# Larger units and larger DMA descriptors in a streaming log-sum-exp scan

## The chip, the cores and the metric

The kernel runs on one core of a Trainium2 chip. The metric is the device time of one execution in microseconds (us); the six runs of the kernel before lie within 0.14% of one another (1250.54 to 1252.28). A profile of one execution is read beside the times.

## The reference

```python
# x: (8, 4096, 2048) float32
out[:, 0, :] = x[:, 0, :]
for t in range(1, 4096):
    mx = np.maximum(out[:, t-1, :], x[:, t, :])
    out[:, t, :] = mx + np.log(np.exp(out[:, t-1, :] - mx) + np.exp(x[:, t, :] - mx))
```

It is a running log-sum-exp along the second axis: 268 MB are read and 268 MB are written. The kernel computes exp, a prefix sum, and log.

## The kernel before: the parts that matter

A tile is 512 rows: 128 partitions, each with R = 4 consecutive rows of 2048 floats, so one partition's share is 32 KiB, contiguous in HBM. The profile shows one DMA packet for each such share (65 loads of 128 data packets and 16 small ones, under 512 B, are the 9360 of queue q1; the small ones come at the end of a transfer and are called its completion packets below); the text below calls its size the descriptor size. There are NI = 6 buffers.

```python
R = 4;  NI = 6
ti = [pool.tile([P, R, D], f32, name=f"ti{i}", tag=f"ti{i}") for i in range(NI)]
...
# SyncE: a buffer is loaded again when its store has landed
take(sp, stored[n], 16)
load(x_v[bass.ds(j * NI + n, 1)][0], n)
...
# ScalarE, tile by tile: exp of tile n, then log of tile n-1, then its store
exp(n, 0);  exp(n, 1)                    # two halves of the columns
ln(n - 1, 0, ...);  ln(n - 1, 1, ...)
store(n - 1, ...)
...
# VectorE: adds row r-1 to row r inside each partition (3 adds a half);
# PE: sums over partitions and the carry from the tile before, into PSUM;
# VectorE: adds that PSUM row to all four rows
```

Loads are issued by SyncE on one DMA queue (q1 in the profile), stores by ScalarE on another (q10). The logarithm of tile n-1, and with it the store, comes after the exponential of tile n, and so after the landing of the load of tile n.

The softmax here doesn't subtract the row's maximum and nothing guards it: scores larger than these inputs give would overflow.

## Time and profile before

| | before |
|---|---|
| median of 6 runs | 1250.79 us |
| share of DMA queues q1 + q10 | 49.9% + 49.9% |
| VectorE / ScalarE / PE busy | 82% / 73% / 52% |
| one tile in the steady state | 19.40 us |
| load / store, issue to landing | 38.4 / 44.0 us |

The lines themselves stand in the prediction. In a group line, the two numbers after the first bar are the total busy time in us and the mean of one instruction in ns; after the second bar come the engine's idle time before them and what ended it. A queue's share is the time that its packets took, as a share of 16 engines over the span.

### The profile page before, as it was taken

The page shows a single profiled execution, that of the slowest core. Times are in us where ns is not written, and L with a number is a line of the kernel's source. Part 1 is how long each engine was busy: PE and PEld are TensorE (multiplying, and loading weights), DVE is VectorE, ACT ScalarE, POOL GpSimd, SP SyncE. Part 2 cuts the span into 40 slices and gives each one's busy share as a digit, 9 for nine tenths or more (in the row PEclk, how much of TensorE's full clock was granted, in tenths as well). Part 3 has the DMA queues.
Part 4 walks back from the last instruction along what each step waited for, and adds up shares of the span by engine and source line. Part 5 has one row for each costly group of instructions (what it writes and reads, how often), then busy time and mean ns, then how long its engine had stood idle before and what let it go on. Part 6 is the DMA issues. An engine that isn't in the chain of part 4 may idle for free. (4 is left out here: it accounts for less than half of the span.)

```text
span 1249.0 us, 3456 instructions
## 1 busy us (share of the span) xinstructions
PE 650.8 (52%) x960; PEld 215.3 (17%) x960; DVE 1023.0 (82%) x512; ACT 907.2 (73%) x258; POOL 1.1 (0%) x8
## 2 busy tenths in 40 slices
PE   3556455554566545655455544565545564465541
PEld 1112111111112111211111111121111121111110
DVE  4999978778787787887878878778787787877873
ACT  5897866867768677686776866867768677686774
POOL 0000000000000000000000000000000000000000
PEclk9897778786887868778778786777878878678785
DMA  9999999999999999999999999999999999999998
GB/s 403 420 436 430 433 430 437 433 431 434 430 436 434 431 433 430 437 434 430 434 430 436 436 430 434 430 436 437 428 434 431 436 436 429 434 430 436 436 430 354
DMA packets 20409, 537.01 MB, mean 430 GB/s; under 512 B 2096, under 2 KB 2096, under 8 KB 4144
## 3 DMA queue, kind: packets, MB, share of 16 engines
q1 hardware_dynamic: 9360, 268.44, 49.9%
q10 hardware_dynamic: 11040, 268.44, 49.9%
q8 instruction: 7, 0.11, 0.0%
q14 instruction: 2, 0.02, 0.0%
HBM read 268.44 MB, written 268.44 MB: 430 GB/s over the span
## 5 line engine op out<-in xcount | busy, mean ns | idle before, releaser
L136 ACT ACTIVATE ti<-ti 128x4096 f32<-128x4096 f32 (+1 forms) x128 | 452.6, 3582 | 310.2 <-ACTq L59 304.2
L232 DVE TENSOR_TENSOR ti<-ti 128x1024 f32<-128x1024 f32 x384 | 464.7, 1224 | 200.0 <-ACT ti L136 191.3
L241 DVE TENSOR_TENSOR ti<-ti,ps 128x4096 f32<-128x4096 f32 x128 | 560.0, 4416 | 9.4 <-PE ps L208 9.0
L208 PE MATMUL ps<-ti,before 128*128 128x512 f32 x512 | 380.4, 895 | 342.6 <-DVE ti L232 342.1
L142 ACT ACTIVATE ti<-ti 128x4096 f32<-128x4096 f32 x128 | 455.4, 3602 | 11.5 <-PE ps L197 6.0
L197 PE MATMUL ps<-ti,last 128*128 128x512 f32 x448 | 270.6, 735 | 234.2 <-DVE ti L241 234.2
L208 PEld LDWEIGHTS ps<-ti,before 128*128 128x128 f32 x512 | 128.7, 279 | 609.0 <-DVE ti L232 500.9
L197 PEld LDWEIGHTS ps<-ti,last 128*128 128x128 f32 x448 | 86.6, 214 | 401.8 <-DVE ti L241 334.7
L159 ACT ACTIVATE ti<-ti 128x4096 f32<-128x4096 f32 x1 | 3.6, 3616 | 6.5 <-ACTq L59 6.5
L32 ACT ACT_TABLE_LOAD x1 | 1.3, 1283 | 0.8 <-PEq L274 0.8
L103 POOL TENSOR_SCALAR_AFFINE_SELECT last<-last 128x128 f32<-128x128 f32 x1 | 0.3, 296 | 0.0
L98 POOL TENSOR_SCALAR_AFFINE_SELECT before<-before 128x128 f32<-128x128 f32 x1 | 0.3, 295 | 0.1
L95 POOL MEMSET last<- 128x128 f32 x1 | 0.2, 206 | 0.0
L94 POOL MEMSET before<- 128x128 f32 x1 | 0.2, 205 | 0.5 <-SPq L77 0.5
L274 POOL MEMSET const-bfloat16-1.0<- 128x1 bf16 x1 | 0.1, 103 | 0.0
L274 POOL MEMSET const-uint8-127<- 128x1 uint8 x1 | 0.1, 103 | 0.0
L274 POOL MEMSET const-float32-0.0<- 128x1 f32 x1 | 0.1, 99 | 0.3 <-issue 0.3
L274 POOL MEMSET const-float32-1.0<- 128x1 f32 x1 | 0.1, 99 | 0.0
## 6 DMA issues: line engine op xcount, KB each, us to landing
ti<-in_x_dram SPq DMA_DIRECT2D x63, 4096.0 KB, 38.4
out_dram<-ti ACTq DMA_DIRECT2D x62, 4096.0 KB, 44.0
out_dram<-ti ACTq DMA_DIRECT2D x4, 2048.0 KB, 12.9
ti<-in_x_dram SPq DMA_DIRECT2D x2, 2048.0 KB, 9.7
```

Of the source, the lines that this page charges most:

```text
L32: nc.scalar.preload_act_table_set("natural_log_exp_and_others")
L94: g.memset(before[:], 1.0).then_inc(ones, 1)
L98: g.affine_select(out=before[:], in_=before[:], compare_op=mybir.AluOpType.is_ge, fill=0.0, base=-1, pattern=[[1, P]], channel_multiplier= ...
L103: g.affine_select(out=last[:], in_=last[:], compare_op=mybir.AluOpType.is_ge, fill=0.0, base=-(P - 1), pattern=[[0, P]], channel_multiplier=1,
L136: act.activation(t[:, rows, half(h)], t[:, rows, half(h)], ACT.Exp).then_inc(exps[h], 1)
L142: act.activation(t[:, :, half(h)], t[:, :, half(h)], ACT.Ln)._wait_ge(carried[h], turn + 1).then_inc(logs, 1)
L159: act.activation(ti[0][:, 0:2, :], ti[0][:, 0:2, :], ACT.Exp)
L197: m = pe.matmul(ps[(n + 1) % 2][:, sl], last[:], ti[n % NI][:, R - 1, sl], start=True, stop=False, skip_group_check=True,)
L208: m = pe.matmul(ps[n % 2][:, sl], before[:], ti[n % NI][:, R - 1, sl], start=n % NBLK == 0, stop=True, skip_group_check=True,)
L232: a = dve.tensor_add(t[:, r, half(h)], t[:, r - 1, half(h)], t[:, r, half(h)])
L241: dve.tensor_add(t[:, :, half(h)], t[:, :, half(h)], ps[n % 2][:, half(h)].unsqueeze(1).to_broadcast([P, R, HALF]),)._wait_ge(ahead[h], n ...
L274: nc = _bacc.Bacc("TRN2", target_bir_lowering=False, num_devices=1)
```

## The change

The intent: units of 1024 rows (eight to a partition) make one partition's share 64 KiB, so that loads and stores need half as many descriptors and semaphore waits. The six buffers become three of twice the size. Only the first four and the last four units have 512 rows. Loops are unrolled on every engine. The first two large units store in two pieces, to free their halves earlier. The core of the diff:

```diff
-    R = 4
-    NI = 6
+    SLOTS, R = 6, 4
+    HEAD, SPLIT, TAIL = 4, 2, 4
+    while row < B * S:
+        r = R if len(units) < HEAD or row >= B * S - TAIL * R * P else 2 * R
+        units.append((row // S, row % S, r, slot))
...
-    ti = [pool.tile([P, R, D], f32, name=f"ti{i}", tag=f"ti{i}") for i in range(NI)]
+    big = [pool.tile([P, 2 * R, D], f32, name=f"big{i}", tag=f"big{i}") for i in range(SLOTS // 2)]
...
+                for u in range(N):
+                    first, _, free = fills[u]
+                    for k, n in free:
+                        sp.wait_ge(stored[k], n)
+                    r = units[u][2]
...
+                        sp.dma_start(
+                            out=sbuf(u, slice(0, r), full), in_=dram(x, u)
+                        ).then_inc(loaded[first], 16)
...
+                for u in range(N):
+                    if u < N - 1:
+                        for h in range(2):
+                            exp(u + 1, h)
+                    ln(u, 0, slice(0, units[u][2]))
+                    own = slots(u)
+                    for i, rows in enumerate(parts(u)):
+                        ln(u, 1, rows)
+                        store(u, rows, stored[own[i % len(own)]])
```

There are 36 units: 4 small, 28 large, 4 small. ScalarE's order is unchanged.

More of the change, by code (lines that the diff above doesn't have):

```diff
@@ L35 @@
     P = 128
-    R = 4
-    NBLK = S // (P * R)
-    NT = B * NBLK
+    SLOTS, R = 6, 4
     FD = 512
-    NI = 6
     HALF = D // 2
-    assert NI % 2 == 0 and NBLK % 2 == 0 and D == 4 * FD
+    HEAD, SPLIT, TAIL = 4, 2, 4
+    assert D == 4 * FD and HEAD % 2 == 0 and TAIL % 2 == 0
+    units = []
+    row = slot = 0
+    while row < B * S:
+        r = R if len(units) < HEAD or row >= B * S - TAIL * R * P else 2 * R
+        units.append((row // S, row % S, r, slot))
+        row += r * P
+        slot = (slot + r // R) % SLOTS
+    N = len(units)
+    assert all(s0 + r * P <= S and sl * R + r <= SLOTS * R for _, s0, r, sl in units)
     pool = ctx.enter_context(tc.tile_pool(name="io", bufs=1))
@@ L47, with dram, sbuf, parts @@
     last = pool.tile([P, P], f32, name="last", tag="last")
-    ti = [pool.tile([P, R, D], f32, name=f"ti{i}", tag=f"ti{i}") for i in range(NI)]
+    big = [pool.tile([P, 2 * R, D], f32, name=f"big{i}", tag=f"big{i}") for i in range(SLOTS // 2)]
     ps = [psum.tile([P, D], f32, name=f"ps{i}", tag=f"ps{i}") for i in range(2)]
-    x_v = x.rearrange("b (k p r) d -> (b k) p r d", p=P, r=R)
-    o_v = out.rearrange("b (k p r) d -> (b k) p r d", p=P, r=R)
+    def dram(t, u):
+        b, s0, r, _ = units[u]
+        return t[b, s0:s0 + r * P, :].rearrange("(p r) d -> p r d", r=r)
+    def sbuf(u, rows, cols):
+        sl = units[u][3]
+        lo = sl % 2 * R
+        return big[sl // 2][:, lo + rows.start:lo + rows.stop, cols]
+    def parts(u):
+        r = units[u][2]
+        n = 2 if u == N - 1 or HEAD <= u < HEAD + SPLIT else 1
+        return [slice(k * r // n, (k + 1) * r // n) for k in range(n)]
+    def slots(u):
+        _, _, r, sl = units[u]
+        return range(sl, sl + r // R)
+    full = slice(0, D)
     def half(h):
         return slice(h * HALF, (h + 1) * HALF)
-    def event(engine, waits, updates):
+    def take(engine, s, n):
         engine.add_instruction(mybir.InstEventSemaphore(
@@ L64, in event @@
                     wait_mode="sem-ge-imm", wait_value=n,
-                ) for s, n in waits],
+                )],
                 on_update=[mybir.SyncUpdate(
                     sync_type="semaphore", id=s.num, ant_name=s.name,
-                    update_mode=mode, update_value=n,
-                ) for s, mode, n in updates],
-            ),
-        ))
-    def take(engine, s, n):
-        event(engine, [(s, n)], [(s, "sem-sub-imm", n)])
+                    update_mode="sem-sub-imm", update_value=n,
+                )],
+            ),
+        ))
     with tc.tile_critical():
@@ L83 @@
         )
-        loaded, stored = sems("loaded", NI), sems("stored", NI)
+        loaded, stored = sems("loaded", SLOTS), sems("stored", SLOTS)
         exps, chain, sums, ahead, joined, carried = (
@@ L88 @@
         )
+        loads, stores, fills = [0] * SLOTS, [0] * SLOTS, []
+        for u in range(N):
+            free = [(k, stores[k]) for k in slots(u) if stores[k]]
+            first = slots(u)[0]
+            loads[first] += 16
+            fills.append((first, loads[first], free))
+            for k, _ in zip(slots(u), parts(u)):
+                stores[k] += 16
+            if len(parts(u)) > len(slots(u)):
+                stores[first] += 16
         with nc.Block() as block:
@@ L106, in _ @@
                 ).then_inc(shaped, 1)
+                take(g, ones, 2)
             @block.sync
             def _(sp):
-                def load(src, n):
-                    sp.dma_start(out=ti[n][:], in_=src).then_inc(loaded[n], 16)
-                sp.dma_start(out=ti[0][:, 0:2, :], in_=x_v[0][:, 0:2, :]).then_inc(top, 16)
-                sp.dma_start(out=ti[0][:, 2:R, :], in_=x_v[0][:, 2:R, :]).then_inc(loaded[0], 16)
-                for n in range(1, NI):
-                    load(x_v[n], n)
@@ L118, in _ @@
-                turns = (NT - NI) // NI
-                with sp.Fori(1, turns + 1) as j:
-                    for n in range(NI):
-                        take(sp, stored[n], 16)
-                        load(x_v[bass.ds(j * NI + n, 1)][0], n)
-                for n in range((turns + 1) * NI, NT):
-                    take(sp, stored[n % NI], 16)
-                    load(x_v[n], n % NI)
-                for n in range(NT - NI, NT):
-                    take(sp, stored[n % NI], 32 if n >= NT - 2 else 16)
+                for u in range(N):
+                    first, _, free = fills[u]
+                    for k, n in free:
+                        sp.wait_ge(stored[k], n)
+                    r = units[u][2]
+                    if u == 0:
+                        for rows, s in ((slice(0, 2), top), (slice(2, r), loaded[first])):
+                            sp.dma_start(
+                                out=sbuf(u, rows, full), in_=dram(x, u)[:, rows, :]
+                            ).then_inc(s, 16)
+                    else:
+                        sp.dma_start(
+                            out=sbuf(u, slice(0, r), full), in_=dram(x, u)
+                        ).then_inc(loaded[first], 16)
@@ L130, in _ @@
             @block.scalar
             def _(act):
-                def exp(n, h, rows=slice(0, R)):
-                    t = ti[n % NI]
-                    if h == 0:
-                        take(act, loaded[n % NI], 16)
-                    act.activation(
-                        t[:, rows, half(h)], t[:, rows, half(h)], ACT.Exp
-                    ).then_inc(exps[h], 1)
-                def ln(n, h, turn):
-                    t = ti[n % NI]
-                    act.activation(
-                        t[:, :, half(h)], t[:, :, half(h)], ACT.Ln
-                    )._wait_ge(carried[h], turn + 1).then_inc(logs, 1)
@@ L146, in store @@
-                def store(n, dst, turn, h=None):
-                    cols = slice(0, D) if h is None else half(h)
-                    act.wait_ge(logs, 2 * turn + (2 if h is None else h + 1))
-                    act.dma_start(
-                        out=dst[:, :, cols], in_=ti[n % NI][:, :, cols]
-                    ).then_inc(stored[n % NI], 16)
-                def settle(turns):
-                    take(act, carried[0], turns)
-                    take(act, carried[1], turns)
-                    take(act, logs, 2 * turns)
@@ L158, in _ @@
-                take(act, top, 16)
-                act.activation(ti[0][:, 0:2, :], ti[0][:, 0:2, :], ACT.Exp)
-                exp(0, 0, slice(2, R))
-                exp(0, 1, slice(2, R))
-                turns = (NT - 2) // NI
-                with act.Fori(0, turns) as j:
-                    for n in range(1, NI + 1):
-                        exp(n, 0)
-                        exp(n, 1)
-                        ln(n - 1, 0, n - 1)
-                        ln(n - 1, 1, n - 1)
-                        store(n - 1, o_v[bass.ds(j * NI + (n - 1), 1)][0], n - 1)
-                    settle(NI)
@@ L171, in _ @@
-                first = turns * NI
-                for n in range(first + 1, NT):
-                    up, turn = n - 1, n - 1 - first
-                    exp(n, 0)
-                    if n < NT - 1:
-                        exp(n, 1)
-                    ln(up, 0, turn)
-                    if n == NT - 1:
-                        store(up, o_v[up], turn, 0)
-                        exp(n, 1)
-                    ln(up, 1, turn)
-                    store(up, o_v[up], turn, 1 if n == NT - 1 else None)
+                done = [0]
@@ new lines, in exp @@
+                def exp(u, h):
+                    first, n, _ = fills[u]
+                    r = units[u][2]
+                    lo = 0
+                    if u == 0:
+                        lo = 2
+                        if h == 0:
+                            piece = sbuf(u, slice(0, lo), full)
+                            act.activation(piece, piece, ACT.Exp)._wait_ge(top, 16)
+                    piece = sbuf(u, slice(lo, r), half(h))
+                    a = act.activation(piece, piece, ACT.Exp)
+                    if h == 0:
+                        a._wait_ge(loaded[first], n)
+                    a.then_inc(exps[h], 1)
@@ new lines, in ln, with store @@
+                def ln(u, h, rows):
+                    piece = sbuf(u, rows, half(h))
+                    act.activation(piece, piece, ACT.Ln)._wait_ge(
+                        carried[h], u + 1
+                    ).then_inc(logs, 1)
+                    done[0] += 1
+                def store(u, rows, s):
+                    act.wait_ge(logs, done[0])
+                    act.dma_start(
+                        out=dram(out, u)[:, rows, :], in_=sbuf(u, rows, full)
+                    ).then_inc(s, 16)
@@ new lines, in _ @@
+                for h in range(2):
+                    exp(0, h)
+                for u in range(N):
+                    if u < N - 1:
+                        for h in range(2):
+                            exp(u + 1, h)
[4 more added lines that the diff above has]
+                        store(u, rows, stored[own[i % len(own)]])
+                take(act, top, 16)
@@ L183, in _, with carry @@
+                for k in range(SLOTS):
+                    if loads[k]:
+                        take(act, loaded[k], loads[k])
                 for h in range(2):
-                    ln(NT - 1, h, NT - 1 - first)
-                    store(NT - 1, o_v[NT - 1], NT - 1 - first, h)
-                settle(NT - first)
+                    take(act, carried[h], N)
+                take(act, logs, done[0])
             @block.tensor
             def _(pe):
-                def carry(n, h):
-                    if n % NBLK == NBLK - 1:
-                        event(pe, [(joined[h], n + 1)], [(carried[h], "sem-add-imm", 1)])
+                def carry(u, h):
+                    r = units[u][2]
+                    if u == N - 1 or units[u + 1][1] == 0:
+                        pe.wait_ge(joined[h], u + 1)
+                        pe.sem_inc(carried[h], 1)
@@ L197, in carry @@
                         m = pe.matmul(
-                            ps[(n + 1) % 2][:, sl], last[:], ti[n % NI][:, R - 1, sl],
+                            ps[(u + 1) % 2][:, sl], last[:], sbuf(u, slice(r - 1, r), sl)[:, 0, :],
                             start=True, stop=False, skip_group_check=True,
@@ L201, in carry, with triangle @@
                         if c == 2 * h:
-                            m._wait_ge(joined[h], n + 1)
+                            m._wait_ge(joined[h], u + 1)
                     m.then_inc(carried[h], 1)
-                def triangle(n, h):
+                def triangle(u, h):
+                    r = units[u][2]
                     for c in range(2 * h, 2 * h + 2):
@@ L208, in triangle @@
                         m = pe.matmul(
-                            ps[n % 2][:, sl], before[:], ti[n % NI][:, R - 1, sl],
-                            start=n % NBLK == 0, stop=True, skip_group_check=True,
+                            ps[u % 2][:, sl], before[:], sbuf(u, slice(r - 1, r), sl)[:, 0, :],
+                            start=units[u][1] == 0, stop=True, skip_group_check=True,
                         )
                         if c == 2 * h:
-                            m._wait_ge(sums[h], n + 1)
+                            m._wait_ge(sums[h], u + 1)
@@ L214, in triangle @@
                     m.then_inc(ahead[h], 1)
-                pe.wait_ge(shaped, 2)
-                for n in range(NT):
+                take(pe, shaped, 2)
+                for u in range(N):
                     for h in range(2):
-                        triangle(n, h)
+                        triangle(u, h)
                     for h in range(2):
-                        carry(n, h)
+                        carry(u, h)
                 for h in range(2):
-                    take(pe, sums[h], NT)
-                    take(pe, joined[h], NT)
+                    take(pe, sums[h], N)
+                    take(pe, joined[h], N)
@@ L227, in _ @@
             @block.vector
             def _(dve):
-                def local(n, h):
-                    t = ti[n]
-                    for r in range(1, R):
-                        a = dve.tensor_add(t[:, r, half(h)], t[:, r - 1, half(h)], t[:, r, half(h)])
-                        if r == 1:
-                            a._wait_ge(exps[h], n + 1)
-                        else:
-                            a._wait_ge(chain[h], (R - 2) * n + r - 1)
-                        a.then_inc(*((chain[h], 1) if r < R - 1 else (sums[h], 1)))
@@ L239, in join @@
-                def join(n, h):
-                    t = ti[n]
-                    dve.tensor_add(
-                        t[:, :, half(h)], t[:, :, half(h)],
-                        ps[n % 2][:, half(h)].unsqueeze(1).to_broadcast([P, R, HALF]),
-                    )._wait_ge(ahead[h], n + 1).then_inc(joined[h], 1)
-                def turn(tiles):
-                    for n in range(tiles):
-                        for h in range(2):
-                            local(n, h)
-                        for h in range(2):
-                            join(n, h)
-                    for h in range(2):
-                        take(dve, exps[h], tiles)
-                        take(dve, chain[h], (R - 2) * tiles)
-                        take(dve, ahead[h], tiles)
@@ L257, in _, with local @@
-                with dve.Fori(0, NT // NI):
-                    turn(NI)
-                turn(NT % NI)
+                steps = [0, 0]
+                def local(u, h):
+                    r = units[u][2]
+                    for k in range(1, r):
+                        row = sbuf(u, slice(k, k + 1), half(h))
+                        a = dve.tensor_add(row, sbuf(u, slice(k - 1, k), half(h)), row)
+                        if k == 1:
+                            a._wait_ge(exps[h], u + 1)
+                        else:
+                            a._wait_ge(chain[h], steps[h])
+                        if k < r - 1:
+                            a.then_inc(chain[h], 1)
+                            steps[h] += 1
+                        else:
+                            a.then_inc(sums[h], 1)
@@ new lines, in join @@
+                def join(u, h):
+                    r = units[u][2]
+                    piece = sbuf(u, slice(0, r), half(h))
+                    dve.tensor_add(
+                        piece, piece,
+                        ps[u % 2][:, half(h)].unsqueeze(1).to_broadcast([P, r, HALF]),
+                    )._wait_ge(ahead[h], u + 1).then_inc(joined[h], 1)
+                for u in range(N):
+                    for h in range(2):
+                        local(u, h)
+                    for h in range(2):
+                        join(u, h)
@@ L263 @@
+                for h in range(2):
+                    take(dve, exps[h], N)
+                    take(dve, chain[h], steps[h])
+                    take(dve, ahead[h], N)
+        for k in range(SLOTS):
+            if stores[k]:
+                take(nc.sync, stored[k], stores[k])
 _INS = ['x']
```

## The prediction

> **What bounds the kernel now.** I read the page first, its utilisation slices and its DMA queues, and then the costliest groups.
>
> ```profile
> DMA  9999999999999999999999999999999999999998
> q1 hardware_dynamic: 9360, 268.44, 49.9%
> q10 hardware_dynamic: 11040, 268.44, 49.9%
> L136 ACT ACTIVATE ti<-ti 128x4096 f32<-128x4096 f32 (+1 forms) x128 | 452.6, 3582 | 310.2 <-ACTq L59 304.2
> L232 DVE TENSOR_TENSOR ti<-ti 128x1024 f32<-128x1024 f32 x384 | 464.7, 1224 | 200.0 <-ACT ti L136 191.3
> L241 DVE TENSOR_TENSOR ti<-ti,ps 128x4096 f32<-128x4096 f32 x128 | 560.0, 4416 | 9.4 <-PE ps L208 9.0
> L142 ACT ACTIVATE ti<-ti 128x4096 f32<-128x4096 f32 x128 | 455.4, 3602 | 11.5 <-PE ps L197 6.0
> ti<-in_x_dram SPq DMA_DIRECT2D x63, 4096.0 KB, 38.4
> out_dram<-ti ACTq DMA_DIRECT2D x62, 4096.0 KB, 44.0
> ```
>
> The DMA engines are full in every slice (49.9% + 49.9%), the busiest compute engine (VectorE) is 82% busy, and ScalarE's idle time, 304 us, ends at a wait inside its own queue, which in the code is the wait for a load. So the DMA engines set the pace. The last two lines give the reserve: a load takes 38.4 us from issue to landing, a store 44.0. To see the rhythm I took the timeline in the middle of the span.
>
> ```profile
> 606.42 7.12 ACT L136 ACTIVATE ti<-ti 128x4096 f32<-128x4096 f32 x2 [5.28 <-ACTq L59]
> 613.45 7.11 ACT L142 ACTIVATE ti<-ti 128x4096 f32<-128x4096 f32 x2
> 620.72 0.34 ACTq L149 DMA_DIRECT2D out_dram<-ti  x1
> 625.82 7.12 ACT L136 ACTIVATE ti<-ti 128x4096 f32<-128x4096 f32 x2 [5.26 <-ACTq L59]
> ```
>
> One tile (4 MiB in, 4 MiB out, 8.39 MB) takes 625.82 - 606.42 = 19.40 us, or 432 GB/s. A tile's store is issued 14.3 us after the exponential of the NEXT tile starts, because ScalarE does the exponential of tile n+1 before the logarithm of tile n. By the landing times, (38.4 + 44.0) / 19.4 = 4.2 transfers are outstanding on average: the six buffers leave always more than one transfer queued, so a queue never runs dry while a store completes and the next load is issued.
>
> What one such turn costs shows only at the start of the span, where it is not hidden:
>
> ```profile
> 1.03 0.39 SPq L114 DMA_DIRECT2D ti<-in_x_dram  x1
> 8.62 3.62 ACT L159 ACTIVATE ti<-ti 128x4096 f32<-128x4096 f32 x1 [6.53 <-ACTq L59]
> 13.50 3.71 ACT L136 ACTIVATE ti<-ti 128x2048 f32<-128x2048 f32 x2 [1.27 <-ACTq L59]
> 63.04 0.34 SPq L111 DMA_DIRECT2D ti<-in_x_dram  x1
> ```
>
> The first 2 MiB load is issued at 1.03 and usable at 8.62, 7.59 us later; the second follows 4.88 us after it, which is the transfer alone. So about 2.7 us are latency at the two ends. Narrow DMA windows split it: first packets start at 2.0 to 2.4 (1.0 to 1.4 us after the issue, and each first packet takes 0.65 us longer than a later one). At the other end, the last small completion packets of the first store start at 62.2 to 62.4, and the load that waits for this store is issued at 63.04, 0.75 us later. From the end of a store's data to the first bytes of a load waiting for it: 0.1 + 0.75 + 1.1 + 0.65 = **2.6 us**, my estimate of a hole.
>
> [...]
>
> **Part by part.**
> (1) Descriptors of 64 KiB. [...] I take -3.
> (2) Straight-line engines: nothing on the path, 0 us.
> (3) VectorE: a unit of eight rows has 14 row additions, two units of four had 12. 28 large units x 2 x 1.224 us = +69 us of busy time. Per unit 14 x 1.224 + 4 x 4.416 = 34.8 us, beside 38.8 us of transfer. Still hidden.
> (4) Three buffers of twice the size. This is the part that counts. In the steady state one unit is 38.8 us of DMA work (19.4 in, 19.4 out). A 128x8192 activation is about 7.0 us (3.6 plus two steps of 1.7, the difference between 128x4096 at 3.61 and 128x2048 at 1.90). Let T be the moment at which load u+2 is usable. Exponential and logarithm take 4 x 7.0 = 28 us, so store u+1 sends its first byte at about T + 29. The load of u+3 needs the buffer of u and so the end of store u. Store u began 29 us after the previous T. Say e us pass between that and T; it had half the rate for that time, and then is alone: it ends at about T + 18.6 - e/2, always before T + 29. At this moment load u+2 has landed, store u+1 isn't issued, load u+3 waits: **no transfer is outstanding**, and all 16 engines stand for 2.6 us. Load u+3 then runs alone until T + 29 and shares after it. That gives a period of 38.8 + 2.6 = 41.4 us.
> The refills that wait so are the loads of large units 7 to 32 (26) and the two pairs of small tail units: 28 x 2.6 = **+73 us**.
> (5) Alternation. With the same times, the next overlap is e' = 25 - e: it neither settles nor grows. Walking the start through by hand (stores 0 to 2 are issued at 38.5, 55.4 and 70.2 as now; load 4 done at 79.7, load 5 at 114, load 6 at 140.6, load 7 at 196) e comes out near 28, beyond the 23 at which a load ends before the next store starts. Then each second period has another hole of 2.3 us: two periods take 77.6 + 5.2 + 2.3 = 85.1, or 42.6 each. Twelve such pairs: **+28 us** at most, and jitter can only lessen it; I take half, +14.
> (6) Ends. The last unit stores rows instead of column halves, the tail has one hole of 2.5 us more, the head one of 0.8: +3 us.
> Sum: 1250.8 - 3 + 73 + 14 + 3 = 1338; as the hand-walk says full alternation (1352) I put it at **1342 us**.
>
> **Rivals.**
> A, the transfers stay hidden (what the change intends). For it: only 28 us of ScalarE and 34.8 us of VectorE stand against 38.8 us of DMA, and three buffers are as many bytes as six. Then -3 us: 1248. Against: a whole unit must be stored before any of its buffer can be refilled, and compute holds (41.4 + 28) / 41.4 = 1.7 of the three buffers, leaving 1.3 for transfers instead of 4.2.
> B, VectorE becomes the bound. Its busy time would be 1023 + 69 = 1092 us of a longer span, 34.8 us a unit against 41.4. It would have to lose another 7 us a unit to waits for ScalarE or PE, and those for PE are 9 us in all now. If so the time is again near 1340 or more, but with the DMA holes longer and ended by a late store.
> C, the hole is smaller because the 16 engines finish at different times, or because both sides overlap: with 1.5 us and no alternation, 1250.8 + 42 = 1293. With 3.2 us and full alternation, 1250.8 + 90 + 28 = 1369.
>
> **Range and chances.** C's two ends are nearly the range: 1302 to 1368. [...] Within 2% (up to 1276) needs a hole under about 1 us or rival A: 0.06. Slower: 0.93.
>
> **What would show it.** In the changed profile the DMA row drops from 9s to about 9 and 8, the two queues sum to about 93%, the rate to about 402 GB/s. In a fine DMA window there is one gap of 2 to 3 us in each period, just before each load of a large unit, and in some periods a second one just before a store. Exponentials start 41 to 43 us apart on average, perhaps 28 and 57 in turn. VectorE is at 1090 us busy, and the load's time to landing falls below 30 us. Had I been wrong on (4), DMA rows would stay at 9 with a period of 38.8; wrong on (1), the rate within a period, gaps left out, would differ from 432 GB/s by more than 1%; with rival B VectorE would have no wait for the exponential.

The chance of a faster time was 0.01. The sum: 1250.8 - 3 + 73 + 14 + 3 = 1338, put at 1342. Its term of -3, and with it the 1248 of rival A, has no working beside it; without it the sum is 1341.

## The result and the profile after

| | before | after |
|---|---|---|
| median of 6 runs | 1250.79 us | 1354.72 us |
| lowest to highest | 1250.54 to 1252.28 | 1351.17 to 1366.24 |
| mean rate over the span | 430 GB/s | 397 GB/s |

The ratio is 1.0839 (95% interval 1.0801 to 1.0878), slower.

From the page of the changed kernel, the utilisation slices, the queues, the groups and the DMA issues (where the last number is the median time from issue to landing, and no size is printed for the large ones):

```profile
DMA  9999999999999999999899989999999999999998
q1 hardware_dynamic: 5328, 268.44, 49.2%
q10 hardware_dynamic: 5616, 268.44, 46.0%
L263 DVE TENSOR_TENSOR big<-big 128x1024 f32<-128x1024 f32 x440 | 535.8, 1224 | 248.4 <-ACT big L177 235.7
L177 ACT ACTIVATE big<-big 128x8192 f32<-128x8192 f32 (+2 forms) x72 | 444.2, 6216 | 426.6 <-DMA big<-in_x_dram 424.5
L277 DVE TENSOR_TENSOR big<-big,ps 128x8192 f32<-128x8192 f32 (+1 forms) x72 | 553.8, 7732 | 0.7 <-PE ps L237 0.7
big<-in_x_dram SPq DMA_DIRECT2D x28, 30.1
out_dram<-big ACTq DMA_DIRECT2D x26, 29.1
```

The packet counts have about halved as intended (q1 from 9360 to 5328, q10 from 11040 to 5616). Nothing else is better. The queues together are busy 95.2% of the span instead of 99.8%; ScalarE waits 424.5 us for loads; VectorE does 440 row additions instead of 384, but its idle time has grown as well (1249.0 - 1023.0 = 226 us before, 1352.2 - 1085.8 = 266 after), so it isn't the bound. The row of nines is misleading: a slice is 34 us long and a digit 9 begins at 90%, so a hole of 2 us in each period hardly shows. By the landing times, (30.1 + 29.1) / 42.7 = 1.4 transfers are outstanding on average, where it was 4.2 (42.7 us is the mean period, below).

The timeline of ScalarE's and SyncE's queues in the middle of the span shows the rhythm:

```profile
601.60 0.34 ACTq L191 DMA_DIRECT2D out_dram<-big  x1
620.88 13.95 ACT L177 ACTIVATE big<-big 128x8192 f32<-128x8192 f32 x2 [19.32 <-DMA big<-in_x_dram]
632.94 0.33 SPq L159 DMA_DIRECT2D big<-in_x_dram  x1
648.70 0.34 ACTq L191 DMA_DIRECT2D out_dram<-big  x1
658.39 13.95 ACT L177 ACTIVATE big<-big 128x8192 f32<-128x8192 f32 x2 [9.72 <-DMA big<-in_x_dram]
675.27 0.33 SPq L159 DMA_DIRECT2D big<-in_x_dram  x1
```

The load of 632.94 waits for the store of 601.60. The next store is issued at 648.70, 28 us after the exponential of 620.88, as in the prediction. Between the landing of the load at about 620 and 632.94 only one transfer is outstanding, the store, and when it ends there is none. The exponentials start 37.5 us apart and then 47 or 49: the turns of step (5) exist, but narrower than predicted here. The mean over the 24 periods from the exponential at 194.31 to that at 1218.74 is 42.7 us.

DMA windows of the changed kernel around the hole and around the joining of the store. A window counts the packets that start in it, and its share is the time these packets take, over 16 engines and the window's length. In order: 632.0 to 632.6, 632.6 to 633.6, 633.6 to 635.0, 649.0 to 650.0 and 651.0 to 652.4.

```profile
DMA packets 16, 0.00 MB, mean 0 GB/s; under 512 B 16, under 2 KB 16, under 8 KB 16
q10 hardware_dynamic: 16, 0.00, 1.5%
...
DMA packets 0, 0.00 MB, mean 0 GB/s; under 512 B 0, under 2 KB 0, under 8 KB 0
...
q1 hardware_dynamic: 15, 0.98, 207.0%
...
q1 hardware_dynamic: 16, 1.05, 242.4%
...
q1 hardware_dynamic: 16, 1.05, 255.7%
```

First come the 16 small completion packets of the store; then a microsecond in which no packet starts anywhere; then the first packets of the load. These last 207.0% x 16 x 1.4 us / 15 = 3.09 us each, where an undisturbed 64 KiB packet (fourth window) lasts 242.4% x 16 x 1.0 us / 16 = 2.42 us. In the fifth window, just before the first packet of the store that was issued at 648.70, a load packet lasts 255.7% x 1.4 us = 3.58 us.

I put such windows of 0.2 us together into mean start times of each round of 16 packets (my own working, not an answer of the profile):

```text
632.31  store's completion packets
634.15  load, first packet    3.05 us   1.84 us empty, then 0.64 us longer than 2.41
637.21 ... 649.26  six load packets, 2.42 us each
651.66  load, eighth packet   3.58 us   1.17 us longer; the store joins
655.25  store, first packet   2.42 us   6.5 us after its issue
657.68 ... 672.19  seven store packets, 2.42 us each
674.60  store's completion packets
```

The period is 674.60 - 632.31 = 42.29 us. Sixteen packets of 2.41 us are 38.6; the empty time (1.84), the slow first packet (0.64) and the slow packet at the joining (1.17) are 3.65; the sum is 42.2. So this period, one from the middle of the span, is explained to 0.1 us. Not every period divides in the same way; step (5) below has the rest.

### The profile page after: what moved, and what is told of

Same layout as the page of the kernel before. It is cut to its first block, busy times and chain, and to the rows that moved or that the text cites. A ratio compares the mean times of both kernels' runs of the same rounds, so it can differ in the third digit from the quotient of the medians.

```text
span 1352.2 us, 1905 instructions
## 1 busy us (share of the span) xinstructions
PE 441.0 (33%) x512; PEld 139.6 (10%) x512; DVE 1085.8 (80%) x512; ACT 894.3 (66%) x149; POOL 1.1 (0%) x8
## 3 DMA queue, kind: packets, MB, share of 16 engines
q1 hardware_dynamic: 5328, 268.44, 49.2%
q10 hardware_dynamic: 5616, 268.44, 46.0%
## 5 line engine op out<-in xcount | busy, mean ns | idle before, releaser
L263 DVE TENSOR_TENSOR big<-big 128x1024 f32<-128x1024 f32 x440 | 535.8, 1224 | 248.4 <-ACT big L177 235.7
L177 ACT ACTIVATE big<-big 128x8192 f32<-128x8192 f32 (+2 forms) x72 | 444.2, 6216 | 426.6 <-DMA big<-in_x_dram 424.5
L277 DVE TENSOR_TENSOR big<-big,ps 128x8192 f32<-128x8192 f32 (+1 forms) x72 | 553.8, 7732 | 0.7 <-PE ps L237 0.7
L237 PE MATMUL ps<-big,before 128*128 128x512 f32 x288 | 247.1, 1009 | 654.7 <-DVE big L263 654.6
L184 ACT ACTIVATE big<-big 128x8192 f32<-128x8192 f32 (+2 forms) x75 | 448.2, 6015 | 11.2 <-PE ps L225 7.6
L225 PE MATMUL ps<-big,last 128*128 128x512 f32 x224 | 194.0, 1016 | 232.6 <-DVE big L277 232.6
L237 PEld LDWEIGHTS ps<-big,before 128*128 128x128 f32 x288 | 78.7, 302 | 824.7 <-DVE big L263 756.9
L225 PEld LDWEIGHTS ps<-big,last 128*128 128x128 f32 x224 | 60.9, 300 | 363.1 <-DVE big L277 310.7
L175 ACT ACTIVATE big<-big 128x4096 f32<-128x4096 f32 x1 | 3.6, 3616 | 6.3 <-DMA big<-in_x_dram 6.3
## 6 DMA issues: line engine op xcount, KB each, us to landing
big<-in_x_dram SPq DMA_DIRECT2D x28, 30.1
out_dram<-big ACTq DMA_DIRECT2D x26, 29.1
```

What stands on the lines that cost most here:

```text
L175: act.activation(piece, piece, ACT.Exp)._wait_ge(top, 16)
L177: a = act.activation(piece, piece, ACT.Exp)
L184: act.activation(piece, piece, ACT.Ln)._wait_ge(carried[h], u + 1).then_inc(logs, 1)
L225: m = pe.matmul(ps[(u + 1) % 2][:, sl], last[:], sbuf(u, slice(r - 1, r), sl)[:, 0, :], start=True, stop=False, skip_group_check=True,)
L237: m = pe.matmul(ps[u % 2][:, sl], before[:], sbuf(u, slice(r - 1, r), sl)[:, 0, :], start=units[u][1] == 0, stop=True, skip_group_check=True,)
L263: a = dve.tensor_add(row, sbuf(u, slice(k - 1, k), half(h)), row)
```

## The experiments

All kernels are edits of the changed one, and all gave correct results. Those with an interval were timed in three rounds; the others are single, beside effects of 3 to 19%.

**Theory H (hole):** three buffers leave so few transfers outstanding that the queues run dry once a unit. **Rivals:** the 64 KiB descriptors themselves; the longer compute chain of eight rows; the straight-line code.

The record also settles a rival that is not in this list. The granted TensorE clock was 0.78 in the profiled run before and 0.60 after. But VectorE waits only 0.7 us for PE in the whole span (line L277 above), and x4 (clock 0.61) and x8 (clock 0.60) below differ by 61 us; so the clock is not the cause.

### x1: straight-line code alone

```diff
-    HEAD, SPLIT, TAIL = 4, 2, 4
+    HEAD, SPLIT, TAIL = 64, 0, 4
```

All units then have 512 rows, in six buffers.

> The changed kernel's straight-line code with every unit at 512 rows: six buffers of 32 KiB a partition, 32 KiB descriptors. If the holes of three big buffers are the cause, none is left: 1248 to 1255 us, period 19.4 us. If the straight-line code or the row-wise last store costs something, it shows here as more than 1260.

Measured: 1250.96 us, ratio 0.9981 (0.9951 to 1.0011). The straight-line code and the new last store neither cost nor gain.

### x2 and x3: the number of buffers, at 32 KiB descriptors

```diff
-    SLOTS, R = 6, 4
-    HEAD, SPLIT, TAIL = 4, 2, 4
+    SLOTS, R = 3, 4            # x3: 4
+    HEAD, SPLIT, TAIL = 64, 0, 4
-    ... for i in range(SLOTS // 2)]
+    ... for i in range((SLOTS + 1) // 2)]
```

> As x1, but only three buffers of 512 rows, so 32 KiB descriptors with three buffers. Hole theory: every one of some 61 refills waits for a store with nothing else queued; 2.4 us of hole and about 1 us when the store joins, 61 x 3.4 = 207: about 1450 us (1400 to 1480), period 22 to 23 us. If 64 KiB descriptors or eight-row units are the cause: 1250.

Measured: 1484.79 us, 234 us more than the kernel before; over 61 refills 3.8 us each, above the 3.4 expected, and just above the range (1400 to 1480). The queues and landing times of x2:

```profile
q1 hardware_dynamic: 9360, 268.44, 48.1%
q10 hardware_dynamic: 9360, 268.44, 41.9%
big<-in_x_dram SPq DMA_DIRECT2D x63, 4096.0 KB, 15.8
out_dram<-big ACTq DMA_DIRECT2D x63, 4096.0 KB, 16.5
```

With (15.8 + 16.5) / 23.0 us = 1.4 transfers outstanding (23.0 is the mean distance of its load issues, from 48.5 to 1430.6 in 60 steps) it stands where the changed kernel stands, and pays about the same per refill with half the descriptor size and half the unit. In its windows a load's first round of packets comes 1.9 us after the store's completion packets and lasts 1.97 us instead of 1.21. This is the strongest evidence for H: neither the size of the descriptor nor that of the unit is needed for the loss.

> As x1 with four buffers of 512 rows. Hole theory: compute holds about 1.7 buffers, 2.3 are left for transfers, and a load is already queued when the store ends: 1250 to 1262 us, period 19.4. If bytes of buffer count and not the number of buffers: far above, 1350 or more.

Measured: 1288.4 us. The direction was right, the size was not: four buffers are not enough. About 0.6 us a refill are left; queues are busy 98.7%. That leaves some 17 us of empty time, where it was 2.5; the packets themselves took about 24 us more in sum (98.7% of 1286.7 us against 99.8% of 1249.0). With (23.0 + 22.4) / 20.1 = 2.3 outstanding, this fits a queue that still runs dry at times and is joined again, but the windows of this run were not taken apart.

### x10: five buffers

The edit is that of x2 with SLOTS = 5.

> As x1 with five buffers of 512 rows. Reserve theory: three gave 1485, four 1288, six 1251; with five about 3.2 transfers are outstanding, a queue hardly runs dry: 1250 to 1258 us.

Measured: 1250.2 us, ratio 0.9993 (0.9966 to 1.0020). Its landing times:

```profile
big<-in_x_dram SPq DMA_DIRECT2D x63, 4096.0 KB, 24.2
out_dram<-big ACTq DMA_DIRECT2D x63, 4096.0 KB, 39.0
```

(24.2 + 39.0) / 19.4 = 3.3 transfers outstanding suffice. The series 3, 4, 5, 6 buffers is 1485, 1288, 1250, 1251 us.

### x4: eight-row units, refilled by halves

```diff
-    HEAD, SPLIT, TAIL = 4, 2, 4
+    HEAD, SPLIT, TAIL = 4, 28, 4       # every large unit stores in two halves
...
-                    for k, n in free:
-                        sp.wait_ge(stored[k], n)
+                        for i in range(r // R):      # loads in halves of four rows
+                            rows = slice(i * R, (i + 1) * R)
+                            for k, n in free:
+                                if k == slots(u)[i]:
+                                    sp.wait_ge(stored[k], n)
+                            sp.dma_start(...[:, rows, :]).then_inc(loaded[first], 16)
```

> The changed kernel with its eight-row units, but both transfers of each large unit in two halves of four rows (32 KiB descriptors), each half of a load waiting only for its own half's store. Hole theory: the second half of the store still runs while the first half of the load is issued, so no hole: 1250 to 1265 us. If the length of the compute chain of eight-row units (VectorE, ScalarE) is the cause: about 1350 still.

Measured: 1292.51 us, ratio 1.0319 (1.0283 to 1.0354), with units, engines' work and SBUF as in the changed kernel. 62 us of the 104 are gone, so the eight-row compute chain is not the cause of these. But the expected 1265 was missed by 28 us. The queues of x4:

```profile
q1 hardware_dynamic: 9360, 268.44, 50.5%
q10 hardware_dynamic: 9360, 268.44, 48.7%
```

They are busy 99.2%, so hardly any empty time is left; packets take longer at times instead (a round of load packets before a store joins lasts 1.83 us, not 1.21). In the profiled run, the fastest of the four (1282.68 us), about 24 of the 32 us above the kernel before are longer packets and 8 are empty time. What the three slower runs lose beyond that is not shown.

### x5 and x6: which direction's descriptors?

x5 takes only the first line of x4's edit (stores in halves). x6 halves only the loads, and both halves wait for the whole store:

```diff
+                        for i in range(r // R):
+                            rows = slice(i * R, (i + 1) * R)
-                        sp.dma_start(out=sbuf(u, slice(0, r), full), in_=dram(x, u)).then_inc(...)
+                            sp.dma_start(out=sbuf(u, rows, full), in_=dram(x, u)[:, rows, :]).then_inc(...)
```

> The changed kernel with only the stores of large units in two halves of four rows (32 KiB descriptors); loads stay whole with 64 KiB and wait for both halves. Hole theory: the load still waits for the whole store with nothing else queued: 1335 to 1355 us. If 64 KiB store descriptors are the cause: about 1300 or less.

Measured: 1345.61 us, as H expects: half the store descriptor size moves the time by 0.7% (the changed kernel: 1354.72).

> The changed kernel with only the loads of large units in two halves of four rows (32 KiB descriptors), both waiting for the whole 64 KiB store. Hole theory: 1340 to 1357 us. If 64 KiB load descriptors are the cause: about 1300 or less.

Measured: 1432.51 us. Neither theory had this. The timeline of x6:

```profile
593.71 13.95 ACT L179 ACTIVATE big<-big 128x8192 f32<-128x8192 f32 x2 [0.42 <-ACT big L186]
656.70 13.95 ACT L179 ACTIVATE big<-big 128x8192 f32<-128x8192 f32 x2 [35.20 <-DMA big<-in_x_dram]
```

and that of x5:

```profile
618.38 13.95 ACT L177 ACTIVATE big<-big 128x8192 f32<-128x8192 f32 x2 [13.81 <-DMA big<-in_x_dram]
660.82 13.95 ACT L177 ACTIVATE big<-big 128x8192 f32<-128x8192 f32 x2 [14.03 <-DMA big<-in_x_dram]
```

x5 is steady at 42.4 us. x6 goes in turns of 63 and 28 us, 91 for two units. In x6's windows beside a store, 32 KiB load packets (1.21 us) and 64 KiB store packets (2.42 us) alternate one to one, so the load has a third of the time there, 1.21 of 3.63 us. The sizes of x5, the other way round, also occur in the changed kernel, whose first small stores run beside large loads. There the load has two thirds (window 43.0 to 57.5, 64 data packets of each queue; the 80 of q1 include 16 small ones):

```profile
q1 hardware_dynamic: 80, 4.19, 66.8%
q10 hardware_dynamic: 64, 2.10, 33.5%
```

In x6, once the store is done, the load has the engines alone, and then they stand: the last load packets end at 676.8, the next store is issued at 684.52, after the logarithms, and no packet starts between 677.0 and 685.2. This gave a new theory for these kernels, **S (share):** the queue with the larger packet takes the larger share, and a favoured store drives the alternation of step (5) to its extreme.

### x8 and x9: the test of the share

x8 is x6 with the stores halved too. x9 is x6 with loads in quarters (two rows, 16 KiB).

> As x6, with the stores of large units in halves of four rows too, so both queues hold 32 KiB descriptors; each load still waits for both halves of the store. Share theory: the engines alternate one packet of each queue, so in x6 a 64 KiB store packet took two thirds of the rate beside a 32 KiB load packet, loads landed late and in turns; with equal packets this goes, and what is left is the hole and the joining of the store, as in the changed kernel: 1335 to 1360 us. If halving the loads is itself the cost: 1400 or more, like x6.

Measured: 1353.31 us. Equal packets bring back the time of the changed kernel (1354.72). Halving the loads was not the cost. It is also the cleanest test of the descriptor size, since every large transfer waits as in the changed kernel: 32 KiB both ways, 1353; 64 KiB both ways, 1355.

x8 is also x4 with only the waits changed back: in x4 each half of a load waits for its own half's store, in x8 for the whole one. The times are 1292.51 (lowest to highest 1282.68 to 1294.90) and 1353.31 us. So at equal units, equal descriptors and equal stores the whole-unit wait costs about 61 us. That is the direct test of H on the large units.

> As x6 with the loads in quarters (16 KiB descriptors) beside whole 64 KiB stores. Share theory: a load beside a store gets a fifth of the rate, so the turns get no better: 1430 to 1520 us, exponentials in turns of 28 us and over 60. If x6 was slow for another reason than the share: about 1432 or less, without such turns.

Measured: 1459.48 us, with exponentials 28.2 and 63.0 us apart in turn, as S expects. In its windows a 16 KiB load packet (0.61 us) and a 64 KiB store packet (2.42 us) alternate.

### x7: 64 KiB descriptors without the whole-unit wait

Each large transfer becomes two DMAs, the even and the odd partitions; a load of a lane waits only for the store of the same lane.

```diff
+    lanes = (slice(0, P, 2), slice(1, P, 2))
...
+                            sp.dma_start(
+                                out=sbuf(u, slice(0, r), full)[ps_], in_=dram(x, u)[ps_]
+                            ).then_inc(loaded[first], 16)
```

> The changed kernel with 64 KiB descriptors both ways, but each large transfer in two DMAs, the even and the odd partitions, each load of a lane waiting only for the store of the same lane. Hole theory: as with halves by rows, 1245 to 1265 us. If 64 KiB descriptors are the cause: about 1350 still.

Measured: 1341.49 us, ratio 1.0728 (1.0707 to 1.0750). My expectation fell. The timeline shows why it isn't a verdict for the descriptor size:

```profile
618.23 13.95 ACT L188 ACTIVATE big<-big 128x8192 f32<-128x8192 f32 x2 [26.98 <-DMA big<-in_x_dram]
646.05 1.13 ACTq L218 DMA_DIRECT2D out_dram<-big  x2
647.22 13.95 ACT L188 ACTIVATE big<-big 128x8192 f32<-128x8192 f32 x2 [1.21 <-issue]
702.15 13.95 ACT L188 ACTIVATE big<-big 128x8192 f32<-128x8192 f32 x2 [27.14 <-DMA big<-in_x_dram]
```

Turns of 29 and 55 us: the alternation is at its extreme. In the windows of this pair, the load is complete at 644.6 and the store's first packets come at 647.3, 2.7 us in which no packet moves, which is the second hole of step (5); and where the load later joins the stores, two rounds of packets last 3.1 and 3.8 us instead of 2.4. The first hole is gone, the second one and the joinings are there. Together with x8 the picture is consistent, but x7 alone doesn't tell the two apart.

x4 has turns nearly as wide (28.8 and 50 us) and hardly a hole. A difference of the two edits besides the descriptor size is when the store starts. x4 issues its first half after half of the second logarithm:

```profile
592.43 13.95 ACT L180 ACTIVATE big<-big 128x8192 f32<-128x8192 f32 x2 [22.65 <-DMA big<-in_x_dram]
616.84 0.34 ACTq L194 DMA_DIRECT2D out_dram<-big  x1
```

That is 24.4 us after the exponential; in x7 it is 27.8 us. A store that starts 3.4 us earlier (27.8 - 24.4) would by this estimate close a hole of 2.7 us. This is argued from the two timelines; no run tests it.

No kernel in the series beats the one before; x10 equals it with one buffer less. A version that keeps 64 KiB descriptors with more buffers was not tried; three of them take 3 x 64 = 192 KiB of a partition.

## Why the prediction was right, point by point

- **The bound:** right. The transfers bound both kernels: the queues are busy 99.8% and 95.2% of the span, VectorE, the busiest compute engine, 82% and 80%.
- **(1) Descriptors, -3 us:** a guess, and the effect is as small as that. A 64 KiB packet takes 2.42 us where two of 32 KiB take 2 x 1.21; by rounds of 16 packets a unit moves in about 38.6 us against 38.8, some 4 us over 28 units. x8 against the changed kernel (1353.31, a single run, against 1354.72) shows no gain at all.
- **(2) Straight-line, 0 us:** shown by x1.
- **(3) VectorE still hidden:** right; 1085.8 us busy against the 1092 worked out, and 235.7 us of its idle time end at ScalarE's exponential, so rival B is out.
- **(4) A hole at each refill:** right in place and size. The store ends before the next is issued, and 1.84 us empty plus 0.64 us of slow first packet are 2.48 us where 2.6 were estimated. x2 shows it at another size. Rival A fails with it. The half rate that the working of (4) takes for two transfers side by side is seen in the kernel before: 50.1% for each queue in the window 606.0 to 625.4.
- **(5) Alternation:** the turns were right, the price was taken from the wrong place. "Then each second period has another hole of 2.3 us" is the step that failed. In the middle of the span the turns are 37.6 and 47.5 us and there is no second hole. From 880 us on they widen to 29 and 57, but the gap there is only 0.4 us (load complete at 909.1, store's first packets at 909.4). In its place stands a term that I didn't have: where a store joins a running load, a round of packets takes 1.17 us longer. Up to 860 us this is paid in each period (0.5 to 1.4 us); in the extreme turns mostly in each second one (1.2 us at 940, 1026 and 1110, under 0.1 at 909, 995 and 1080). There, a straggling packet can add to a hole: at 929 one of the store's 16 completion packets starts at 930.6, the other 15 at 928.7 to 928.9, and from these 15 to the load's first packets it is 3.6 us instead of 1.8.

  I had +14 us for this step. The queues' shares give what it was over the whole span (estimates, since the shares are rounded): 4.8% of 1352.2 us, 65 us, are empty where 0.2% of 1249.0, 2.5 us, were, and the packets took 41 us more in sum. Of these 62 + 41 us, 28 x 1.84 = 52 and 28 x 0.64 = 18 are step (4). Some 33 are left for step (5): about 23 of longer packets, the joining, and 10 of longer holes.
- **(6) Ends, +3 us:** not measured by itself.
- **The sum:** with the middle's period for all 28 units, 28 x 3.65 = 102, less 4 for (1), gives 1349; measured 1354.7. The central 1342 was low mainly by step (5), +14 instead of some 33. The hand-walk's 1352 came close partly by luck, since its second hole stood in for the joining.
- **The signs named in advance:** the queues' sum was put at 93% and is 95.2%, the rate at 402 and is 397 GB/s; the DMA row hardly leaves 9, since slow packets count as busy and the slices are long. The load's landing was to fall below 30 us and is 30.1. The gap before a load was to be 2 to 3 us and is 1.84; the turns of 28 and 57 us did come, late in the span.
- **A slip in the working, on which nothing rests:** the 18.6 of (4) is not worked out there, and 19.4 - e/2 follows from what it says; "always before T + 29" holds with either.

## What to carry to other kernels

Count the transfers that stay outstanding, (load latency + store latency) / period, before making a unit larger: in a chain where the store of one unit waits for the load of the next, 1.4 lost a hole per refill, 2.3 some, 3.3 nothing, and doubling the unit at equal memory took this kernel from 4.2 to 1.4. Doubling the descriptor from 32 to 64 KiB gained nothing measurable here (1353.31 us in x8, a single run, against 1354.72). Where two queues share the engines, look at the packet sizes of both. Here 64 KiB store packets beside 32 KiB loads cost 78 us (x6, 1432.51, against the changed kernel, 1354.72), and 64 KiB load packets beside 32 KiB stores nothing (x5, 1345.61).
